# First feed-forward block: down products as seven block products over chunks of six features, norm factor on the gated features

## The chip, the core and the metric

The kernel runs on one core of a Trainium2 chip. Its engines work side by side, each with its own queue in order: TensorE (PE) multiplies matrices into PSUM, VectorE (DVE) and ScalarE (ACT) work element by element, GpSimd (POOL) here issues the DMAs that accumulate into SBUF, SyncE (SP) issues the others. The metric is the time of one execution in device microseconds; lower is better.

## What is computed

The reference is one step of a hybrid decoder: a first half-step SwiGLU block, a mixer (causal pooling beside a state-space part), a second half-step SwiGLU block and a last norm. There are 512 prompt tokens and 8 sample tokens, 520 in all, D_MODEL = 1024 and FFN_DIM = 2816, all in float32. Cut to what matters here:

```python
def _rms_norm(x, g):
    y = xf * lax.rsqrt(jnp.mean(xf * xf, axis=-1, keepdims=True) + EPS)
    return y * g
def _swiglu(x, wg, wu, wd):
    return (jax.nn.silu(x @ wg) * (x @ wu)) @ wd
...
h = h + 0.5 * _swiglu(_rms_norm(h, ffn1_norm[l]), ffn1_w_gate[l], ffn1_w_up[l], ffn1_w_down[l])
```

## The kernel before

Features lie on the 128 partitions and tokens along the free axis. A block of 128 rows is called a feature here: the model has 8 of them, the FFN 22 (f = 0 to 21). The 520 tokens are cut into two halves of 260. `h` (line 81) holds the residual stream in SBUF.

**A product in three matmuls.** Weights and inputs are split into a high part (rounded to fp32r) and a low part (what is left). `mm3` (line 122) adds high x high, high x low and low x high in PSUM, at lines 123, 126 and 127: three matmuls of 128x128 by 128x260. `split` (line 102) makes the parts: ScalarE casts the high part (line 107), VectorE subtracts for the low part (line 114). With `late`, half of the low part is made without VectorE: ScalarE writes the negated high part (line 110) and a DMA from POOL's queue adds the weights from memory onto it (line 111).

**Gate and up.** The norm's factor per token (`nx[3]`, tile `r_f`) isn't put on the input; the matmuls work on h times the norm's weights, and the factor is multiplied on behind. For each feature the gate and up rows form a 2x2 block matrix (gate or up; first or second four input blocks), and so does the input (first or second four blocks; token half). `product` computes the 2x2 by 2x2 product with seven block products instead of eight, numbered 1 to 7, each four input blocks x 3 = 12 matmuls: 84 a feature. `prep_pair` (line 191) makes the seven combinations of the input once, in the tiles `xth` and `xtl`. `load` (line 255) fetches the two weight rows of a feature and makes the combinations of weights: `s1` (line 266) and `s2` (267, 268), then splits the tiles whi/wlo (three buffers a tag) and shi/slo (two). The results gather in the PSUM tiles `A` (one bank, two buffers) and `BE` (two banks, two buffers); ScalarE copies four intermediate sums to `ac` (line 294) before the bank is accumulated further. `gates` (line 298) combines them, applies the factor and Silu and multiplies with one up half; `close` (line 305) does the other half after product 4, and splits the gated feature into `g` (lines 309, 310). `step` runs the products of a feature in the order 1, then product 4 and `close` of the feature before, then 5, 6, 3, 7, 2, then `gates`.

**The first two features** of the first block (f = 0 and 1) are done with plain float32 matmuls (`plain`, line 238) while the inputs arrive; `plain_out` gates them.

**Down.** `rest` goes over the features in chunks of 8, 8 and 6. One or two products of the next chunk's first features come ahead, so that TensorE has work while the last gated feature is split. `down` then takes each of the eight output row blocks d: one load of its weight rows over the chunk (`load_unit`), a split, 2 halves x n features x 3 matmuls into a `BE` tile (named `dn`), then VectorE multiplies with -0.5 and the norm factor (line 364, tile `td`) and adds to `h` (line 368; in the last chunk 371 for each half, followed by the preparation of the mixer's input). The down matmuls of the first block are 22 x 8 x 2 x 3 = 1056.

**Order.** The program is written in the order above; a planner sets the order on each engine by priority (program order, raised by `high_priority`) and by a timeline of its own. Tiles of one tag share buffers, and a new tile waits for the release of an old one. The second block has the same class, chunks of 8, 8 and 6 and another last chunk (`down_by_half`).

Of the kernel before, what the change touches and what calls it, by code (L numbers as in the profile page):

```python
# [33 lines left out]
CHUNKS = (8, 8, 6)  # L34
# [28 lines left out]
def tile_trunk_step(ctx: ExitStack, tc: tile.TileContext, ins: dict, outs: dict):  # L63
# [120 lines left out]
    def scaled(gp, nb, norm, j, name):  # L184
        xg = gp.tile([P, 4, HB], F32, tag="g", bufs=nb, name=f"xg_{name}{j}")
# [5 lines left out]
    def prep_pair(nx, gp, nb, xg, j, name):  # L191
        xth, xtl, _, _ = nx
        xd = gp.tile([P, 4, HB], F32, tag="g", bufs=nb, name=f"xd_{name}{j}")
# [10 lines left out]
    class Ffn:  # L204
# [4 lines left out]
        def __init__(self, nx, i, wx, gp, direct):  # L209
            self.nx, self.i, self.wx, self.gp, self.direct = nx, i, wx, gp, direct  # L210
            self.states = None
            self.w, self.A, self.BE, self.ac, self.g, self.tg, self.raw, self.banks, self.behind = ({} for _ in range(9))

# [12 lines left out]
        def plain(self, f, xg, j, us=(0, 1)):  # L226
            for u in us:
                if (f, u) not in self.banks:
                    n = f"P{self.i}_{f}{u}"
                    if f == 1 and u == 0:  # L230
# [10 lines left out]
        def plain_out(self, f):  # L241
            tg = self.wx.tile([P, 2, HB], F32, tag="tg", bufs=2, name=f"tg{self.i}_{f}")
            g = self.g[f] = self.gp.tile([P, 2, 2, HB], F32R, tag="g", bufs=NG, name=f"g{self.i}_{f}")
# [3 lines left out]
            nc.scalar.activation(out=tg, in_=tg, func=AF.Silu)  # L247
            for b in range(2):
                nc.vector.scalar_tensor_tensor(out=tg[:, b], in0=self.banks[f, 1][b][:, :HB], scalar=-1.0, in1=tg[:, b],
                                               op0=ALU.mult, op1=ALU.mult)  # L250
            nc.scalar.copy(g[:, 0], tg)
            nc.vector.tensor_tensor(out=g[:, 1], in0=tg, in1=g[:, 0].bitcast(F32), op=ALU.subtract)
            return free.ins

        def load(self, f):
            i, wx, src = self.i, self.wx, ins[f"w{self.i}gu"]
            n = f"{i}_{f}"
            raw = raw_pair(n)
            nc.sync.dma_start(out=raw[:, 0], in_=src[2 * f])
            nc.sync.dma_start(out=raw[:, 1], in_=src[2 * f + 1])  # L260
            d1 = split(raw[:, 0], 1024, f"{n}a", wp, 3, ("whi", "wlo"), src[2 * f, :, 512:])
            s1 = wx.tile([P, 2, 512], F32, tag="sw", bufs=2, name=f"s1_{n}")
            s2 = wx.tile([P, 2, 512], F32, tag="sw", bufs=2, name=f"s2_{n}")
            up0 = raw[:, 1, :512].unsqueeze(1).to_broadcast([P, 2, 512])
            diag = bass.AP(up0.tensor, up0.offset - 1024, [up0.ap[0], (1536, 2), up0.ap[2]])
            nc.vector.tensor_tensor(out=s1, in0=diag, in1=up0, op=ALU.add)  # L266
            nc.vector.tensor_tensor(out=s2[:, 0], in0=s1[:, 1], in1=raw[:, 0, :512], op=ALU.add)
            nc.vector.tensor_tensor(out=s2[:, 1], in0=s2[:, 0], in1=raw[:, 0, 512:], op=ALU.add)
            e1 = split(s1.rearrange("p q c -> p (q c)"), 1024, f"{n}c", wx, 2, ("shi", "slo"))
            e2 = split(s2.rearrange("p q c -> p (q c)"), 1024, f"{n}d", wx, 2, ("shi", "slo"))  # L270
            d2 = split(raw[:, 1, 512:], 512, f"{n}b", wp, 3, ("whi", "wlo"), src[2 * f + 1, :, 512:])
            self.w[f] = {1: (d1, 0), 2: (d1, 4), 7: (e1, 0), 5: (e1, 4), 6: (e2, 0), 3: (e2, 4), 4: (d2, 0)}

        def product(self, f, p):
            js = range(KD // 2)
            if f not in self.A:
                with tc.issue_after(self.behind[f]) if f in self.behind else nullcontext():
                    self.load(f)
                n = f"{self.i}_{f}"
                self.A[f] = ps[0].tile([P, 512], F32, tag="A", bufs=2, name=f"A{n}")  # L280
                self.BE[f] = ps[0].tile([P, 2, 512], F32, tag="BE", bufs=2, name=f"BE{n}")
                self.ac[f] = [self.wx.tile([P, 2, HB], F32, tag="ac", bufs=3, name=f"ac{n}_{q}") for q in range(2)]
            slot, dst, opens = {1: (0, 0, True), 2: (1, 1, True), 5: (3, 2, True), 6: (5, 0, False),
                                3: (2, 2, False), 7: (4, 0, False), 4: (6, 0, False)}[p]
            out = self.A[f] if dst == 0 else self.BE[f][:, dst - 1]
            (whi, wlo), k0 = self.w[f][p]
            xth, xtl = self.nx[:2]
            for j in js:
                mm3(out[:, :HB], ws(whi, k0 + j), ws(wlo, k0 + j), xth[:, j, slot], xtl[:, j, slot], opens and j == 0,
                    j == KD // 2 - 1, skip_group_check=True)  # L290
            a, c = self.ac[f]
# [6 lines left out]
        def gates(self, f):  # L298
            tg = self.tg[f] = self.wx.tile([P, 2, HB], F32, tag="tg", bufs=2, name=f"tg{self.i}_{f}")
            nc.vector.tensor_tensor(out=tg, in0=self.BE[f][:, :, :HB], in1=self.ac[f][0], op=ALU.add)  # L300
            nc.vector.tensor_tensor(out=tg, in0=tg, in1=self.nx[3].rearrange("p (b t) -> p b t", b=2), op=ALU.mult)
            nc.scalar.activation(out=tg, in_=tg, func=AF.Silu)
            nc.vector.tensor_tensor(out=tg[:, 1], in0=self.ac[f][1][:, 0], in1=tg[:, 1], op=ALU.mult)

        def close(self, f):
            tg = self.tg[f]
            nc.vector.tensor_tensor(out=tg[:, 0], in0=self.A[f][:, :HB], in1=tg[:, 0], op=ALU.mult)
            g = self.g[f] = self.gp.tile([P, 2, 2, HB], F32R, tag="g", bufs=NG, name=f"g{self.i}_{f}")
            nc.scalar.copy(g[:, 0], tg)  # L309
            nc.vector.tensor_tensor(out=g[:, 1], in0=tg, in1=g[:, 0].bitcast(F32), op=ALU.subtract)  # L310
# [3 lines left out]

        def rest(self, before, last_chunk):
            lo = 0
            for c, n in enumerate(CHUNKS):
                hi = lo + n
                last = hi == KF
                for f in range(self.direct if c == 0 else lo + 1, hi if last else hi + 1):  # L320
                    self.step(f)
                if last:
                    self.product(KF - 1, 4)
                    with tc.high_priority():
                        self.close(KF - 1)
                    wd = before()
                else:
                    self.product(hi + 1, 1)
                    self.product(hi, 4)
                    self.close(hi)  # L330
# [4 lines left out]
                lo = hi  # L335

        def step(self, f):
            if f not in self.A:
                self.product(f, 1)
            if f - 1 not in self.g and f > self.direct:  # L340
                self.product(f - 1, 4)
                self.close(f - 1)
# [772 lines left out]
```

## Time and profile before

| | |
|---|---|
| median of 3 runs | 1008.37 us (1007.89 to 1009.1) |
| profiled execution | 1008.41 us, of which the span is 1006.5 us |
| down products of the first block, in the span | 112 to 371 us |
| first seven-product feature of the second block begins | 651 us |
| HBM traffic | 127.36 MB read, 7.34 MB written |

In the profile, a row of a group reads: line, engine, operation, output tile <- input tiles, shapes, count | busy us, mean ns of one | idle time of the engine before them and who ended it. Rows of the timeline read: start, duration, engine, line, operation, tiles, shapes, and in brackets the idle time before it. Durations of TensorE and VectorE are pipelined: the next instruction can start before the last has ended, so the price of one is the distance between starts. Tile names carry the feature: `slo_5c` is the low part of the first weight sum of feature 5, `shi_5d` the high part of the second.

### The profile page before, as it was taken

What the parts mean: (1) busy time and instruction counts of PE and PEld (TensorE: products, weight loads), DVE (VectorE), ACT (ScalarE), POOL (GpSimd) and SP (SyncE); (2) the same over time, 40 slices, a digit from 0 to 9 for tenths busy, and PEclk for the clock granted to TensorE, in tenths of its full rate; (3) what the DMA queues carried; (4) which work ended last, traced back from release to release, by engine and by line L of the source; (5) the groups of instructions that cost most, each with busy time, mean ns of one, the idle gap of its engine ahead of it and who ended that gap; (6) DMA issues with size and microseconds to landing.
All of it is one profiled execution on the core that took longest, in us unless ns stands there. A gap on an engine that the chain in (4) does not pass through costs nothing.

```text
span 1006.5 us, 19720 instructions
## 1 busy us (share of the span) xinstructions
PE 976.0 (97%) x7852; PEld 952.8 (95%) x7852; DVE 766.7 (76%) x1366; ACT 564.4 (56%) x961; POOL 157.3 (16%) x239
## 2 busy tenths in 40 slices
PE   7999999999999999999999999999999999999996
PEld 6899999999999999999899998899999999999995
DVE  7788556886468688789979987998857788477776
ACT  7677415765137455685754325677644676535653
POOL 0111001110011000156411000111212211122100
PEclk9999999999999999999999999999999999999998
DMA  5566424754345332263335322456646766556612
GB/s 185 166 167 163 111 99 116 178 137 117 126 110 135 93 124 97 90 192 100 121 122 159 117 86 95 127 131 175 140 139 185 210 151 165 131 179 171 144 64 85
DMA packets 53835, 135.97 MB, mean 135 GB/s; under 512 B 7720, under 2 KB 14824, under 8 KB 53744
## 3 DMA queue, kind: packets, MB, share of 16 engines
q1 hardware_dynamic: 38864, 103.78, 31.8%
q0 software_dynamic: 14880, 30.94, 16.0%
q8 instruction: 61, 1.00, 0.4%
q14 instruction: 30, 0.25, 0.1%
HBM read 127.36 MB, written 7.34 MB: 134 GB/s over the span
## 4 chain that ended last, share of the span: by engine, by line
PE 85%; DVE 6%; ACT 5%; issue 2%; DMA 2%; POOL 1%; SPq 0%; DVEq 0%; ACTq 0%; POOLq 0%
PE A L123 8%; PE A L126 7%; PE A L127 7%; PE dn L127 7%; PE dn L123 6%; PE dn L126 6%; PE BE L123 6%; PE BE L127 6%; PE BE L126 6%; PE P L238 3%; PE wo L123 2%; PE wo L126 2%; PE wo L127 2%; PE inz L123 2%; PE inz L127 2%
## 5 line engine op out<-in xcount | busy, mean ns | idle before, releaser
L123 PE MATMUL dn<-g,whi_1d 128*128 128x260 f32 x352 | 99.5, 283 | 1.8 <-ACT whi_1d L107 1.6
L126 PE MATMUL dn<-g,whi_1d 128*128 128x260 f32 x352 | 99.5, 283 | 0.0
L127 PE MATMUL dn<-g,wlo_1d 128*128 128x260 f32 x352 | 99.0, 282 | 0.0
L364 DVE SCALAR_TENSOR_TENSOR td<-dn,r_f 128x520 f32<-128x520 f32 x40 | 27.9, 699 | 91.7 <-PE dn L127 91.7
L127 PE MATMUL dn<-g,wlo_2d 128*128 128x260 f32 x256 | 72.8, 284 | 2.0 <-DVE wlo_2d L114 2.0
L123 PE MATMUL dn<-g,whi_2d 128*128 128x260 f32 x256 | 72.4, 283 | 0.1
L126 PE MATMUL dn<-g,whi_2d 128*128 128x260 f32 x256 | 72.3, 282 | 0.0
L123 PEld LDWEIGHTS dn<-g,whi_1d 128*128 128x128 f32 x352 | 66.1, 188 | 2.4 <-ACT whi_1d L107 2.0
L126 PEld LDWEIGHTS dn<-g,whi_1d 128*128 128x128 f32 x352 | 66.3, 188 | 0.0
L127 PEld LDWEIGHTS dn<-g,wlo_1d 128*128 128x128 f32 x352 | 66.1, 188 | 0.0
L107 ACT CAST whi_1d<-raw_1d 128x1024 fp32r<-128x1024 f32 (+1 forms) x24 | 23.4, 979 | 70.4 <-PE dn L126 62.2
L294 ACT COPY ac<-A 128x260 f32<-128x260 f32 x123 | 44.0, 371 | 17.1 <-PE A L127 17.1
L266 DVE TENSOR_TENSOR s<-raw 128x1024 f32<-128x1024 f32 x41 | 49.9, 1218 | 3.3 <-DMA raw<-in_w2gu 3.3
L238 PE MATMUL P<-xg_f,raw 128*128 128x260 f32 x192 | 45.6, 396 | 5.3 <-DMA raw<-in_w1gu 5.3
L127 PEld LDWEIGHTS dn<-g,wlo_2d 128*128 128x128 f32 x256 | 48.2, 188 | 2.6 <-DVE wlo_2d L114 2.6
L123 PEld LDWEIGHTS dn<-g,whi_2d 128*128 128x128 f32 x256 | 48.3, 189 | 0.3 <-ACT whi_2d L107 0.3
L126 PEld LDWEIGHTS dn<-g,whi_2d 128*128 128x128 f32 x256 | 48.2, 188 | 0.0
L238 PEld LDWEIGHTS P<-xg_f,raw 128*128 128x128 f32 x192 | 37.4, 198 | 11.2 <-ACT xg_f L187 5.2
L126 PE MATMUL wo<-catg,whi_wo 128*128 128x260 f32 x128 | 36.4, 285 | 1.3 <-DVE catg L972 1.3
L123 PE MATMUL wo<-catg,whi_wo 128*128 128x260 f32 x128 | 37.3, 292 | 0.3 <-DVE h L941 0.3
L310 DVE TENSOR_TENSOR g<-tg,g 128x520 fp32r<-128x520 f32 x41 | 28.6, 698 | 11.6 <-ACT g L309 11.6
L123 PE MATMUL inz<-xh_mx,whi_inz 128*128 128x260 f32 x128 | 36.8, 287 | 0.1
(1442 smaller groups left out, 4001.2 us busy)
## 6 DMA issues: line engine op xcount, KB each, us to landing
raw<-in_w2gu SPq DMA_DIRECT2D x44, 512.0 KB, 4.7
raw<-in_w1gu SPq DMA_DIRECT2D x42, 512.0 KB, 4.5
raw_1d<-in_w1d SPq DMA_DIRECT2D x16, 512.0 KB, 4.4
raw_2d<-in_w2d SPq DMA_DIRECT2D x16, 512.0 KB, 5.7
raw_wo<-in_w_out SPq DMA_DIRECT2D x12, 512.0 KB, 4.5
ab<-scr_acs SPq DMA_DIRECT2D x8, 512.0 KB, 4.4
h<-in_state_ssm SPq DMA_DIRECT2D x16, 256.0 KB, 4.1
raw_inz<-in_w_in SPq DMA_DIRECT2D x8, 512.0 KB, 4.3
```

The source lines that it names most:

```text
L107: nc.scalar.copy(h, src)
L123: first = nc.tensor.matmul(ps, whi, xhi, start=start, stop=False, **kw)
L126: nc.tensor.matmul(ps, whi, xlo, start=False, stop=False, **kw)
L127: nc.tensor.matmul(ps, wlo, xhi, start=False, stop=stop, **kw)
L238: nc.tensor.matmul(self.banks[f, u][b][:, :HB], ws(self.raw[f][:, u], j + 4 * q), xg[:, slot[q]], start=j == q == 0, stop=j == 3 and q == ...
L266: nc.vector.tensor_tensor(out=s1, in0=diag, in1=up0, op=ALU.add)
L294: nc.scalar.copy(keep, out[:, :HB])
L310: nc.vector.tensor_tensor(out=g[:, 1], in0=tg, in1=g[:, 0].bitcast(F32), op=ALU.subtract)
L364: nc.vector.scalar_tensor_tensor(out=t, in0=banks[d][:, :, :HB], scalar=-0.5, in1=self.nx[3].rearrange("p (b t) -> p b t", b=2), op0=ALU.mult,
```

## The change

The down products of the first block are done in chunks of six, three times, and a last chunk of four. In the chunks of six, two output row blocks d and d+1 and the two halves of the chunk's features (first three, last three) form a 2x2 block matrix, as gate and up do, and the features by token halves the other; the same seven products give both output blocks, 7 x 3 x 3 matmuls for what took 2 x 2 x 6 x 3. Such a unit (c, d) passes through the same `load`, `product`, `gates` and `close` as a feature; its columns are 768 instead of 1024. Features of a chunk are taken in pairs (0 and 3, 1 and 4, 2 and 5), and after the second of a pair is closed `g_split` makes the seven combinations of the pair and splits them into a tile `gt` (14 parts, three buffers). The first of a pair keeps its gated values in the tile tagged `acc`. The plain features are 0 and 3.

The norm factor and the 0.5 move: each gated feature is multiplied with the factor once more, and the eviction of the down products only adds or subtracts. The last chunk of four stays with plain down products. Input tiles of the plain features move to a pool `xo` of their own, which is released before the pool of the gated features opens. The second block has `paired` = 0, its chunks as before.

```diff
-CHUNKS = (8, 8, 6)
+CHUNKS = {1: (6, 6, 6, 4), 2: (8, 8, 6)}
...
+        def role(self, f):
+            c = self.chunk[f]
+            fs = self.chunks[c]
+            if c < self.paired:
+                return ("first", "second")[fs.index(f) % 2]
+            return "late" if 0 < c <= self.paired and f == fs[0] else "plain"
+
+        def g_homes(self, f):
+            t = self.tg[f]
+            if self.role(f) in ("first", "late"):
+                t = act.tile([P, NT], F32, tag="acc", name=f"gx{self.i}_{f}").rearrange("p (b t) -> p b t", b=2)
+                self.gx = t
+            self.out[f] = t
...
+        def g_split(self, f):
+            role = self.role(f)
+            if role == "plain":
+                self.g_plain(f, self.out[f])
+            if role != "second":
+                return
+            gx, go = self.gx, self.out[f]
+            self.gx = None
+            t = self.gt[f] = self.gp.tile([P, 14, HB], F32R, tag="gt", bufs=3, name=f"gt{self.i}_{f}")
+            xd = self.gp.tile([P, 4, HB], F32, tag="xd", name=f"gd{self.i}_{f}")
+            nc.vector.tensor_tensor(out=xd[:, 0], in0=gx[:, 0], in1=gx[:, 1], op=ALU.subtract)
+            nc.vector.tensor_tensor(out=xd[:, 1], in0=go[:, 1], in1=gx[:, 1], op=ALU.subtract)
+            nc.vector.scalar_tensor_tensor(out=xd[:, 2], in0=xd[:, 1], scalar=-1.0, in1=gx[:, 0], op0=ALU.mult,
+                                           op1=ALU.subtract)
+            nc.vector.scalar_tensor_tensor(out=xd[:, 3], in0=xd[:, 2], scalar=-1.0, in1=go[:, 0], op0=ALU.mult,
+                                           op1=ALU.subtract)
+            for x, q in ((gx[:, 0], 0), (go, slice(1, 3)), (xd, slice(3, 7))):
+                hi, lo = t[:, 0:7][:, q], t[:, 7:14][:, q]
+                nc.scalar.copy(hi, x)
+                nc.vector.tensor_tensor(out=lo, in0=x, in1=hi.bitcast(F32), op=ALU.subtract)
...
+            if self.paired:
+                nc.vector.tensor_tensor(out=tg, in0=tg, in1=self.halves(self.nx[3]), op=ALU.mult)
...
+            if isinstance(k, tuple):
+                c, d = k
+                fs = self.chunks[c]
+                n, src = f"{i}d{d}_{c}", ins[f"w{i}d"][d : d + 2, :, min(fs) * P : (max(fs) + 1) * P]
+            else:
+                n, src = f"{i}_{k}", ins[f"w{i}gu"][2 * k : 2 * k + 2]
+            nb = src.shape[2] // 2
...
+            n = len(self.chunks[k[0]]) // 2 if isinstance(k, tuple) else KD // 2
+            for j in range(n):
+                if isinstance(k, tuple):
+                    t = self.gt[self.chunks[k[0]][2 * j + 1]]
+                    xhi, xlo = t[:, slot], t[:, 7 + slot]
...
+            nc.vector.tensor_tensor(out=tg, in0=self.BE[k][:, :, :HB], in1=a, op=ALU.add)
+            if isinstance(k, tuple):
+                hd, hn = h[:, k[1]], h[:, k[1] + 1, HALVES[1]]
+                nc.vector.tensor_tensor(out=hd, in0=hd, in1=tg.rearrange("p b t -> p (b t)"), op=ALU.add)
+                nc.vector.tensor_tensor(out=hn, in0=hn, in1=c[:, 0], op=ALU.subtract)
+                return
...
+            if self.paired:
+                nc.vector.tensor_tensor(out=tg, in0=tg, in1=r, op=ALU.mult)
+            self.up(k, 1, c[:, 0])
...
+        def close(self, k):
+            if isinstance(k, tuple):
+                hn = h[:, k[1] + 1, HALVES[0]]
+                nc.vector.tensor_tensor(out=hn, in0=hn, in1=self.A[k][:, :HB], op=ALU.subtract)
+                return
+            self.up(k, 0, self.A[k][:, :HB])
+            self.g_split(k)
...
+                if c < self.paired:
+                    for d in range(0, KD, 2):
+                        self.step((c, d))
+                    continue
...
+        def step(self, k):
+            if k not in self.A:
+                self.product(k, 1)
+            self.flush()
+            for p in (2, 5, 6, 3, 7) if k == KF - 1 else (5, 6, 3, 7, 2):
+                self.product(k, p)
+            self.gates(k)
+            self.pending = k
...
+                if self.paired:
+                    if after is None:
+                        nc.vector.tensor_tensor(out=hd, in0=banks[d][:, :, :HB], in1=hd, op=ALU.add)
+                        return
+                    for b, hs in enumerate(HALVES):
+                        nc.vector.tensor_tensor(out=h[:, d, hs], in0=banks[d][:, b, :HB], in1=h[:, d, hs], op=ALU.add)
+                        after(d, b, hs)
+                    return
...
-    wx1, g1 = pool("wx1", "right"), pool("g1", "right")
+    wx1, xo = pool("wx1", "right"), pool("xo", "left")
...
-    ffn1 = Ffn(nx1, 1, wx1, g1, 2)
+    ffn1 = Ffn(nx1, 1, wx1, None, 2, 3)
...
+    xo.release()
+    g1 = ffn1.gp = pool("g1", "right")
```

`flush` runs product 4 and `close` of the feature or unit before; `up` multiplies a gated half with an up half (with -0.5 in the first block); `g_plain` splits one feature as `close` did before.

More of the change, by code (lines that the diff above doesn't have):

```diff
@@ L253, in plain_out @@
+            self.g_split(f)
             return free.ins
-        def load(self, f):
-            i, wx, src = self.i, self.wx, ins[f"w{self.i}gu"]
-            n = f"{i}_{f}"
-            raw = raw_pair(n)
[L259 to L272, printed above, removed]
@@ L312, in scales, with flush @@
         def scales(self):
             rstds(self.nx, f"f{self.i}")
-        def rest(self, before, last_chunk):
[L316 to L320, printed above, removed]
-                    self.step(f)
+        def flush(self):
+            if self.pending is not None:
+                self.product(self.pending, 4)
+                self.close(self.pending)
+                self.pending = None
@@ L459, in tile_trunk_step @@
         for j in range(KD // 2):
-            ffn1.plain(1, xg1[j], j, (u,))
+            ffn1.plain(second, xg1[j], j, (u,))
+    xo.release()
+    g1 = ffn1.gp = pool("g1", "right")
     with tc.high_priority():
-        ffn1.behind[2] = ffn1.plain_out(0)
-    ffn1.plain_out(1)
+        ffn1.behind[ffn1.order[2]] = ffn1.plain_out(0)
+    ffn1.plain_out(second)
     nx2, xa = [], []
```

162 lines of the change are left out of this document (101 added, 61 removed).

## The prediction

> **What bounds the kernel now.** I read the page from the top, then the stretches of the first block by window, then one feature step on VectorE instruction by instruction.
>
> ```profile
> span 1006.5 us, 19720 instructions
> PE 976.0 (97%) x7852; PEld 952.8 (95%) x7852; DVE 766.7 (76%) x1366; ACT 564.4 (56%) x961; POOL 157.3 (16%) x239
> ...
> PEclk9999999999999999999999999999999999999998
> ...
> L123 PE MATMUL dn<-g,whi_1d 128*128 128x260 f32 x352 | 99.5, 283 | 1.8 <-ACT whi_1d L107 1.6
> ```
>
> TensorE is busy for 97% of the span at the full granted clock, so a matmul removed is time removed, unless another engine then runs out. The first block's down products are 1056 matmuls: this group of 352 and its two equals from lines 126 and 127 (three matmuls make one product). Their 283 ns is a pipelined duration; the price of one is the distance between starts:
>
> ```profile
> 362.89 0.70 DVE L364 SCALAR_TENSOR_TENSOR td<-dn,r_f 128x520 f32<-128x520 f32 x1 [0.20 <-PE dn L127]
> ...
> 367.20 0.70 DVE L364 SCALAR_TENSOR_TENSOR td<-dn,r_f 128x520 f32<-128x520 f32 x1 [0.53 <-PE dn L127]
> ```
>
> These two evictions follow the 36 matmuls of one output row block each (6 features x 2 halves x 3): 4.31 us / 36 = 0.120 us. The next view says how full the engines are (PE, PEld, DVE, ACT, POOL, clock, DMA share, GB/s): a stretch of feature steps, the two passages from feature steps to down products, and a stretch of down products.
>
> ```profile
> 65.00:89.00 24.00, 24.00 (x202) 24.00 (x201) 20.50 (x29) 16.78 (x29) 4.33 (x5) 1.00 0.65 155
> 107.00:124.00 17.00, 15.55 (x125) 14.93 (x125) 8.77 (x12) 6.54 (x10) 0.87 (x1) 1.00 0.32 82
> 124.00:150.00 26.00, 26.00 (x219) 26.00 (x219) 12.08 (x15) 4.20 (x4) 0.00 (x0) 1.00 0.33 120
> 236.00:254.00 18.00, 16.55 (x133) 15.93 (x132) 8.70 (x12) 6.54 (x10) 0.87 (x1) 1.00 0.35 97
> ```
>
> In the feature steps TensorE has no idle time at all, and VectorE is already busy for 85% (20.50 of 24). In the down products VectorE is half idle. At each passage TensorE stands for 1.45 us. The VectorE queue over one feature step:
>
> ```profile
> 64.95 1.23 DVE L114 TENSOR_TENSOR slo_5c<-s,shi_5c 128x1024 fp32r<-128x1024 f32 x1 [1.14 <-ACT shi_5c L107]
> 66.10 0.69 DVE L300 TENSOR_TENSOR tg<-BE,ac 128x520 f32<-128x520 f32 x1
> 66.71 1.22 DVE L266 TENSOR_TENSOR s<-raw 128x1024 f32<-128x1024 f32 x1
> 67.84 0.70 DVE L301 TENSOR_TENSOR tg<-tg,r_f 128x520 f32<-128x520 f32 x1
> 68.45 1.22 DVE L114 TENSOR_TENSOR slo_5d<-s,shi_5d 128x1024 fp32r<-128x1024 f32 x1
> 69.58 0.43 DVE L296 TENSOR_TENSOR ac<-ac 128x260 f32<-128x260 f32 x1
> 69.92 0.69 DVE L267 TENSOR_TENSOR s<-s,raw 128x512 f32<-128x512 f32 x1
> 70.53 0.43 DVE L303 TENSOR_TENSOR tg<-ac,tg 128x260 f32<-128x260 f32 x1
> 71.21 0.43 DVE L307 TENSOR_TENSOR tg<-A,tg 128x260 f32<-128x260 f32 x1 [0.26 <-PE A L127]
> 71.55 0.68 DVE L268 TENSOR_TENSOR s<-s,raw 128x512 f32<-128x512 f32 x1
> 72.17 0.69 DVE L114 TENSOR_TENSOR wlo_6a<-raw,whi_6a 128x512 fp32r<-128x512 f32 x1
> 73.22 0.70 DVE L310 TENSOR_TENSOR g<-tg,g 128x520 fp32r<-128x520 f32 x1 [0.36 <-ACT g L309]
> 75.06 1.23 DVE L114 TENSOR_TENSOR slo_6c<-s,shi_6c 128x1024 fp32r<-128x1024 f32 x1 [1.14 <-ACT shi_6c L107]
> ```
>
> The step takes 75.06 - 64.95 = 10.11 us, which is 84 matmuls x 0.120. VectorE idles 0.26 + 0.36 + 1.14 = 1.76 us of it and works 8.35. That 1.76 us is what the change has to live on.
>
> **The change part by part.**
>
> *Matmuls.* A pair of output blocks over six features took 2 x 2 x 6 x 3 = 72 matmuls and takes 7 x 3 x 3 = 63. Four pairs in three chunks: 12 x 9 = 108 fewer, x 0.120 = **13.0 us off**. The last chunk of four stays as it was, 24 matmuls a block. Gate and up products and the whole second block keep their counts.
>
> *The passages.* These rows say what TensorE waits for between 95 and 255 us:
>
> ```profile
> PE dn L123 <- ACT whi_1d L107: 1.6, 2, 0.8
> PE A L123 <- ACT ac L294: 1.4, 4, 0.4
> ```
>
> They come about because products 1 and 4 of the features at the edge run back to back, and because the down weights join the rotation of the weight buffers there. After the change a down unit passes through the same step as a feature, product by product, so both passages should close: 2 x 1.45 = **2.9 us off**; the other end is that nothing closes, 0. The passage into the last chunk remains.
>
> *VectorE in the feature steps.* Each feature gets one more multiplication by the norm factor (a row like L301, 0.61 us from start to start: 67.84 to 68.45). Each pair loses two L310 rows (0.70 each, drained) and gains four sums and three low parts. Their prices stand in the preparation of the input, which does the same work:
>
> ```profile
> 20.25 0.42 DVE L196 SCALAR_TENSOR_TENSOR xd_f<-xd_f,xg_f 128x260 f32<-128x260 f32 x1
> 20.59 1.24 DVE L202 TENSOR_TENSOR xtl_f<-xd_f,xth_f 128x1040 fp32r<-128x1040 f32 x1
> 21.74 0.43 DVE L198 SCALAR_TENSOR_TENSOR xd_f<-xd_f,xg_f 128x260 f32<-128x260 f32 x1
> ```
>
> A 260 costs 0.34, a 1040 1.15, a 520 0.61: 4 x 0.34 + 0.34 + 0.61 + 1.15 = 3.46 us. A pair of steps: 2 x 8.35 - 2 x 0.70 + 2 x 0.61 + 3.46 = 19.98 us against 20.22 us of TensorE. VectorE is then 99% full. The work is not due at once, though: the split of a pair is first read by the down products, and its feature's buffer is needed again two steps later. What is due is the weights' low part. These rows of TensorE, one step earlier, say when:
>
> ```profile
> 58.26 0.28 PE L127 MATMUL BE<-xth_f,slo_4c 128*128 128x260 f32 x1
> ...
> 59.34 0.28 PE L127 MATMUL BE<-xth_f,slo_4c 128*128 128x260 f32 x1
> ...
> 61.15 0.28 PE L123 MATMUL BE<-xth_f,shi_4d 128*128 128x260 f32 x1
> ```
>
> slo_5c ends at 66.18 and its first reader, a step after slo_4c's, starts at 58.26 + 10.11 = 68.37; so it may come 2 us late. The split falls into the flush after L307, at 71.55: laid out there it moves slo_6c by about 1 us, and the following step, which has no split, takes this back. Bounds for a pair: 0, if the order is that good, and 2.5 us, if all of the present idle time but the 0.36 and a little more stays (below). I take 0.3, near the lower end because of the 2 us; 8 pairs in steps: **2.4 us on**.
>
> *VectorE and ScalarE in a down unit.* It carries the weight sums of a feature step over 768 columns: 1.13 x 3/4 = 0.87 for the first sum and for each of two low parts, 0.46 for the two halves and the short low part, then 0.34 (c), 0.61 + 0.61 + 0.34 + 0.34 to combine and add to h: 6.2 us, in 63 x 0.120 = 7.56 us. That share, 82%, is what feature steps carry today with no idle TensorE. Before it was L364, L368 and one low part a block. But the gaps in which ScalarE must empty a bank shrink by a quarter:
>
> ```profile
> 69.81 0.38 ACT L294 COPY ac<-BE 128x260 f32<-128x260 f32 x1 [0.32 <-PE BE L127]
> ```
>
> In the TensorE rows above, between the last matmul of product 5 and the first of product 3 into the same bank lie 1.81 us (59.34 to 61.15), less 0.28 for its end: 1.53 us for this 0.38 us copy. In a unit three matmuls fewer lie between, 1.17 us. Bounds: 0 and 0.6 us a unit (a cast in front of the copy each time); I take 0.15, as it fits if ScalarE has no cast going; 12 units: **1.8 us on**.
>
> *DMA and queues.* SyncE issues two weight loads a unit, as for a feature (8 loads a chunk as before, in four chunks instead of three), and POOL two accumulating loads that the down products did not have:
>
> ```profile
> 66.76 0.87 POOL L111 DMA_DIRECT2D wlo_5b<-in_w1gu  x1 [3.03 <-ACT wlo_5b L110]
> ```
>
> A feature step issues two of these as well, and its DMA share of 0.65 leaves TensorE without a wait; a unit moves three quarters of the bytes in three quarters of the time. I cost it at nothing. The cover is the 7.56 us of the unit before, by which the loads run ahead; without it a unit would start late by what a load lacks. POOL, at 16%, has nothing queued behind.
>
> *The last chunk.* A block falls from 4.31 to 24 x 0.120 = 2.88 us. VectorE worked 4.31 - 0.20 - 0.53 = 3.58 us in the period shown above; it loses L364 (0.61) and a third of a 768 low part (0.29): 2.68 of 2.88. Two banks allow one block of lateness, and in-projection starts on early blocks. Bounds 0 and 2; I take **0.6 us on**.
>
> *Start.* The plain steps now do features 0 and 3 and free their input tiles before the new buffers open. Two more factors and one split land where VectorE had nothing to do, 0 within 1 us:
>
> ```profile
> 40.07 0.69 DVE L114 TENSOR_TENSOR wlo_3a<-raw,whi_3a 128x512 fp32r<-128x512 f32 x1 [1.79 <-ACT whi_3a L107]
> ```
>
>
> **Sum**, against the profiled execution's 1008.4 us (1006.5 in the span and 1.9 around it; the median of the runs is 1008.37): 1008.4 - 13.0 - 2.9 + 2.4 + 1.8 + 0.6 = **997.3 us**.
>
> **Rivals.**
>
> *VectorE becomes the bound (slower).* The place is the pair of feature steps. If the waits of a step that are tied to the order of the products (0.26 and 1.14) stay where they are, a pair needs 19.98 + 2.8 = 22.8 us, 2.6 over TensorE. 8 x 2.6 = 21 in place of 2.4: 1008.4 - 15.9 + 21 + 2.4 = 1016. It decides from (15.9 - 2.4) / 8 = 1.7 us a pair upward. For it: 99% is no margin, and the queue runs in order. Against: those idles exist because nothing else was ready; the split is ready work. Chance 0.10.
>
> *Each instruction pays its full duration.* The twelve durations of the step shown add up to 9.11 us. A pair is then 18.22 - 1.40 + 1.40 + (5 x 0.42 + 0.70 + 1.24) = 22.3 us, 2.0 over TensorE: 1008.4 - 15.9 + 16 + 2.4 = 1011, slower too. Against it: slo_5c starts at 64.95 and lasts 1.23, yet the next row starts at 66.10, 0.08 before its end, and so do nearly all. For it: the three sums of a split that hang on each other do wait in full. Chance 0.04. The Trainium skill ("VectorE: DVE Perf Modes", "The DRAIN you can't avoid") states this rule: the next VectorE operation starts only when the one before has left the pipe, so that the count of operations is to be kept small. By that rule the time would be the 1011 of this rival; the trace agrees only in part, with the 0.08 us.
>
> *The split is laid badly,* 1.2 us a pair: 9.6 for 2.4, 1004.5. For it: in the flush it comes ahead of weight parts that are due sooner. Chance 0.07.
>
> *ScalarE's copies are late in the units:* 0.6 x 12 = 7.2 for 1.8: 1002.7. For it: every unit leaves a quarter less room, and casts of the split join the queue. Against: ScalarE has 56% to do. Chance 0.12.
>
> *All hides:* 1008.4 - 15.9 = 992.5. The feature steps of today show no idle TensorE at 85%. Chance 0.12.
>
> *The passages stay* (the 2.9 remain, or the down units wait for the last split instead): 1000.2; it lies in the forecast's own range and has its chance there.
>
> **How the numbers follow.** The forecast, 994 to 1001.5, has 0.55. With "all hides", the ScalarE case and the badly laid split, 992 to 1005 would hold 0.86; of that some 0.04 falls outside at the two ends. A difference of 0.2%, 2.0 us, is about what can be told from no change. Faster than 1006.4: 0.55 + 0.12 + 0.12 + 0.04 = 0.83. Within: 0.03, the rest of the badly laid split. Slower: 0.10 + 0.04 = 0.14.
>
> **What would show it.** The down matmuls of the first block fall to 192, with 756 in the new units; the unit repeats every 7.6 us and the feature pair every 20.2. The two windows of passages show TensorE full. VectorE in the feature steps reads 95% or more. If a feature pair takes 21 us or more with TensorE waiting for slo or wlo, the first rival holds; if units take over 8 us with waits for ac, the ScalarE one. The prediction would be wrong if TensorE's idle time in the first block passed 10 us, or if a step of the second block changed its length.

## The result and the profile after

The changed kernel takes 999.08 us (median of 4 runs, 996.41 to 999.47) against 1008.25 us for the kernel before (4 runs, one more than in the table above); ratio 0.9902, 95% interval 0.9884 to 0.992. That is 9.2 us faster; 11.1 us were forecast, and the time lies in the range. The profiled execution of the changed kernel took 999.47 us, 997.6 of them in the span.

The page of the changed kernel, its span, engines and clock:

```profile
span 997.6 us, 19913 instructions
PE 963.4 (97%) x7744; PEld 939.7 (94%) x7744; DVE 826.2 (83%) x1509; ACT 614.5 (62%) x1074; POOL 178.5 (18%) x263
...
PEclk9999999999999999999999999999999999999998
```

There are 7852 - 7744 = 108 matmuls fewer, as counted, and VectorE works 60 us more at a share of 83% instead of 76%. What became of the down products, by groups of TensorE's instructions (the first from 36 to 372 us, the second from 84 to 124 us):

```profile
L123 PE MATMUL dn<-gt,whi_1d 128*128 128x260 f32 x64 | 18.1, 285 | 0.8 <-ACT gt L248 0.6 <-DVE h L474 0.3
```

```profile
L123 PE MATMUL A1d<-gt,whi_1d_0a 128*128 128x260 f32 x12 | 3.5, 292 | 0.2 <-DVE gx L395 0.2
```

64 in each of the three lines of a product, 192 in all, are the plain products of the last chunk; the second group shows the first line of one product, over the four units of a chunk (3 pairs x 4).

Two marks in the chain of waits let the gain be placed: the norm sum that ends the first block, and the last input preparation before the second. Before:

```profile
376.09 0.44 PE psr_mx L169 x2
...
647.11 1.06 ACT xth_f L201
```

After:

```profile
365.68 0.44 PE psr_mx L169 x2
...
635.79 1.06 ACT xth_f L202
```

So 10.4 us come from the first block; at the second mark the lead is 11.3 us; at the end it is 1006.5 - 997.6 = 8.9. In the second block, whose instructions did not change, 2.4 us are lost again. There TensorE waits longer for down weights; before, and after (engine, waited for: us in total, times, longest):

```profile
PE dn L127 <- DVE wlo_2d L114: 2.0, 3, 0.8
```

```profile
PE dn L127 <- DVE wlo_2d L114: 4.5, 4, 1.7
```

The first block by stretches, after (TensorE, weight load, VectorE, ScalarE, GpSimd busy; clock; DMA share; GB/s):

```profile
44.00:84.00 40.00, 40.00 (x334) 40.00 (x334) 38.03 (x59) 29.00 (x49) 6.93 (x8) 1.00 0.60 145
84.00:94.00 10.00, 8.73 (x70) 8.29 (x69) 9.87 (x19) 6.66 (x11) 1.73 (x2) 1.00 0.52 118
94.00:124.00 30.00, 29.72 (x245) 29.32 (x245) 25.36 (x41) 21.03 (x40) 6.06 (x7) 1.00 0.70 172
164.00:187.00 23.00, 22.24 (x182) 21.83 (x181) 21.33 (x36) 15.98 (x29) 4.33 (x5) 1.00 0.53 119
187.00:216.00 29.00, 29.00 (x245) 29.00 (x244) 25.91 (x43) 20.47 (x38) 6.06 (x7) 1.00 0.71 175
256.00:280.00 24.00, 23.24 (x190) 22.83 (x190) 22.18 (x38) 16.54 (x30) 4.33 (x5) 1.00 0.54 120
336.00:370.00 34.00, 31.51 (x255) 30.14 (x254) 28.49 (x63) 21.50 (x47) 0.73 (x3) 1.00 0.32 107
```

In feature steps (44 to 84) VectorE is 95% busy and TensorE has no idle time. In the units (187 to 216) none either. TensorE stands at the three passages into the units, 1.27 + 0.28, 0.76 and 0.76 us, and in the last chunk, 2.49 us. Its waits from the first block to the start of the mixer, by what ended them:

```profile
PE BE1d L123 <- ACT gt L269: 1.0, 1, 1.0
PE BE1d L126 <- DVE gt L270: 0.9, 2, 0.5
PE BE1d L123 <- ACT ac1d L367: 0.8, 3, 0.3
PE dn L123 <- ACT gt L248: 0.6, 1, 0.6
PE dn L126 <- DVE gt L249: 0.3, 1, 0.3
PE dn L123 <- DVE h L474: 0.3, 1, 0.3
PE dt L752 <- DVE dt_v L772: 1.4, 1, 1.4
```

The 2.49 us of the last chunk fall into two places: 0.58 + 0.29 + 0.26 = 1.13 us at its start, for the split of a feature and an eviction, and 1.36 us at its end, where the mixer's first product `dt` waits while VectorE, busy for 15.78 of 16 us from 346 to 362, is behind with the evictions and the mixer's input. The kernel before has the same two places, with 0.20 and 0.88 us. Before:

```profile
345.34 0.39 PE L123 MATMUL dn<-g,whi_1d 128*128 128x260 f32 x1 [0.20 <-DVE td L364]
372.36 0.29 PE L635 MATMUL dt<-xh_mx,w 128*48 128x260 f32 x1 [0.88 <-DVE td L364]
```

After, the first wait of the start and the one at the end:

```profile
340.56 0.50 PE L123 MATMUL dn<-gt,whi_1d 128*128 128x260 f32 x2 [0.58 <-ACT gt L248]
361.96 0.29 PE L752 MATMUL dt<-xh_mx,w 128*48 128x260 f32 x1 [1.36 <-DVE dt_v L772]
```

At the passages the waits of before, for whi_1d and ac at the edge, are gone. The new ones are for gt, the split of the last gated pair, and 0.28 us each for the first unit's copy ac1d. VectorE's queue at the first passage shows why the split is late:

```profile
84.03 0.42 DVE L395 SCALAR_TENSOR_TENSOR tg<-A,tg 128x260 f32<-128x260 f32 x1
84.37 0.42 DVE L262 TENSOR_TENSOR gd<-tg,gx 128x260 f32<-128x260 f32 x1
...
88.83 0.42 DVE L265 SCALAR_TENSOR_TENSOR gd<-gd,tg 128x260 f32<-128x260 f32 x1
...
90.38 0.69 DVE L389 TENSOR_TENSOR tg<-tg,r_f 128x520 f32<-128x520 f32 x1
...
92.60 1.23 DVE L270 TENSOR_TENSOR gt<-gd,gt 128x1040 fp32r<-128x1040 f32 x1
```

The pair is closed at 84.03. The last of the four sums runs at 88.83 and the last low part at 92.60, 8.6 us later, for the split shares the queue with the sums and low parts of the first down weights and with the gate of the next feature. From 84 to 94 us VectorE is busy for 9.87 of 10. ScalarE adds to the first wait: the last sum is done at 89.25, but its cast starts at 90.89, behind a cast of weights that starts at 90.15.

### The profile page after: what moved, and what is told of

The parts are those of the page before. It is cut to its first block, busy times and chain, and to the rows that moved or that the text cites. A ratio compares the mean times of both kernels' runs of the same rounds, so it can differ in the third digit from the quotient of the medians.

```text
span 997.6 us, 19913 instructions
## 1 busy us (share of the span) xinstructions
PE 963.4 (97%) x7744; PEld 939.7 (94%) x7744; DVE 826.2 (83%) x1509; ACT 614.5 (62%) x1074; POOL 178.5 (18%) x263
## 4 chain that ended last, share of the span: by engine, by line
PE 81%; DVE 8%; DMA 4%; ACT 3%; issue 2%; POOL 0%; SPq 0%; DVEq 0%; ACTq 0%; POOLq 0%
PE A L123 7%; PE A L126 7%; PE A L127 7%; PE BE L123 6%; PE BE L126 6%; PE BE L127 6%; PE P L296 3%; PE dn L127 2%; PE wo L123 2%; PE dn L126 2%; PE dn L123 2%; PE wo L126 2%; PE wo L127 2%; PE inz L123 2%; DMA raw<-in_w2gu 2%
## 5 line engine op out<-in xcount | busy, mean ns | idle before, releaser
L478 DVE SCALAR_TENSOR_TENSOR td<-dn,r_f 128x520 f32<-128x520 f32 x16 | 11.2, 698 | 32.6 <-PE dn L127 32.6
L107 ACT CAST whi_2d<-raw_2d 128x1024 fp32r<-128x1024 f32 (+1 forms) x18 | 18.5, 1027 | 31.5 <-PE dn L126 16.7
L123 PE MATMUL inx<-xh_mx,whi_inx 128*128 128x260 f32 x128 | 36.4, 284 | 0.0
L127 PE MATMUL wo<-catg,wlo_wo 128*128 128x260 f32 x128 | 36.3, 284 | 0.0
L127 PE MATMUL inx<-xh_mx,wlo_inx 128*128 128x260 f32 x128 | 36.2, 283 | 0.0
L127 PE MATMUL inz<-xh_mx,wlo_inz 128*128 128x260 f32 x128 | 36.2, 283 | 0.0
L126 PE MATMUL inz<-xl_mx,whi_inz 128*128 128x260 f32 x128 | 36.1, 282 | 0.0
L126 PE MATMUL inx<-xl_mx,whi_inx 128*128 128x260 f32 x128 | 36.1, 282 | 0.0
L957 ACT ACTIVATE so<-br,sxdt 128x128 f32<-128x128 f32 x64 | 20.5, 391 | 25.2 <-DMA br<-scr_bc 18.7
```

What stands on the lines that cost most here:

```text
L107: nc.scalar.copy(h, src)
L123: first = nc.tensor.matmul(ps, whi, xhi, start=start, stop=False, **kw)
L126: nc.tensor.matmul(ps, whi, xlo, start=False, stop=False, **kw)
L127: nc.tensor.matmul(ps, wlo, xhi, start=False, stop=stop, **kw)
L478: nc.vector.scalar_tensor_tensor(out=t, in0=banks[d][:, :, :HB], scalar=-0.5, in1=self.nx[3].rearrange("p (b t) -> p b t", b=2), op0=ALU.mult,
L957: nc.scalar.activation(out=o[:, q], in_=br, func=AF.Copy, scale=sxdt[:, j, b : b + 1]))
```

## The experiments

All medians are of runs beside the kernel before on the same chip. Where a run is set against the changed kernel, the changed kernel's own ratio, 0.9902 and 0.9916 in two measurements, is the measure.

**The norm factor alone.** Chunks of 8, 8 and 6, plain products, the factor on the gated features:

```diff
-CHUNKS = {1: (6, 6, 6, 4), 2: (8, 8, 6)}
+CHUNKS = {1: (8, 8, 6), 2: (8, 8, 6)}
...
-            if self.paired:
+            if self.factor:
                 nc.vector.tensor_tensor(out=tg, in0=tg, in1=r, op=ALU.mult)
...
-    ffn1 = Ffn(nx1, 1, wx1, None, 2, 3)
+    ffn1 = Ffn(nx1, 1, wx1, None, 2, 0, True)
```

> Only the norm factor moves onto the gated features; chunks of 8, 8 and 6 and plain down products as before. My theory: a feature step gets 0.61 us of VectorE more (8.35 to 8.96 of 10.1 us), which fits, and a down block loses one eviction of 0.70 us, which was hidden; TensorE's 1056 down matmuls stay, so the time is that of before, 1008.4 within 1.5 us. Rival, the factor itself costs time on a VectorE that is full: 20 features x 0.61 = 12 us slower, 1020. Second rival, the shorter eviction is what gained: 2 to 4 us faster than before.

Measured: 1008.08 us, ratio 0.9992 (0.9983 to 1.0001). By itself this part changes nothing, as the theory had it; the gain belongs to the rest of the change, the units of seven products with their smaller chunks.

**Without the sample states, before and after.** Two runs to separate the second block:

```diff
-    f2["ffn"].states = f2["states"](f2["st"])
-    next(f2["ffn"].states)
```

> The kernel before, leaving out the update of the sample states during the second block (its loads and stores, ScalarE and VectorE work; that output is not written). My theory: the second block, 354.6 us from its first seven-product feature to the end in the trace of before, loses its waits for late weights, 2.0 us or a little more; 1003 to 1007. It is the partner of the next run.

> The changed kernel, leaving out the same update of the sample states. My theory: the 11.3 us that the changed kernel is ahead when the second block begins stay to the end, since the 2.4 us it loses there come from weight loads colliding with the states' DMAs: 11.3 us (10.5 to 12) less than the run without states of the kernel before, and the second block of both equally long within 0.3 us. Rival, the second block itself became slower by the edit: the difference stays 8.9 us.

Measured: 1006.34 us (0.9977, 0.9967 to 0.9987) and 996.34 us (0.9876, 0.9861 to 0.989): 10.0 us apart. The second marks of the two, of the kernel before without states and of the changed one without states:

```profile
647.67 1.06 ACT xth_f L201
```

```profile
637.19 1.06 ACT xth_f L202
```

From there to the ends of the spans (1004.9 and 994.4 us) both take 357.2 us. The lead of 10.5 us at the mark stays to the end. So in this pair of traces the loss in the second block is gone with the states' transfers; the edit doesn't slow that block itself. The difference of the medians, 10.0 us, lies below the 10.5 to 12 that were expected and above the 8.9 of the rival.

**The changed kernel once more.**

> The changed kernel once more. My theory: the first block and the mixer take the same time again to 0.3 us (mixer's start at the same point of the span), and what differs between executions, 996.4 to 999.5 us, lies in the second block, in the waits for wlo of the down weights (4.5 us in the first trace). Rival: the executions differ in the first block.

Measured: 1000.71 us (997.79 to 1001.06), ratio 0.9916 (0.99 to 0.9932). Its norm sum stands at 367.23 us instead of 365.68; the difference is in the start, where TensorE waits 0.8 us for whi_4a, among others. Its second block takes 361.3 us, that of the first trace 361.8, both longer than the 359.4 of the kernel before; in the traces of the runs below, whose edits lie in the first block, it took 360.0 to 364.2. So executions differ in both places, and the expectation that the first block repeats to 0.3 us was wrong.

**More work for VectorE, on the gate's chain.** Once and twice more:

```diff
             nc.vector.tensor_tensor(out=tg, in0=self.BE[k][:, :, :HB], in1=a, op=ALU.add)
+            for _ in range(1 if self.paired and not isinstance(k, tuple) else 0):
+                nc.vector.tensor_tensor(out=tg, in0=self.BE[k][:, :, :HB], in1=a, op=ALU.add)
```

> The changed kernel with the addition of BE and ac (a 520-column VectorE instruction, 0.61 us from start to start) done a second time in every feature step of the first block. My theory: the changed kernel still has about 1.0 us of idle VectorE in a pair of steps (38.03 of 40 us busy), so 1.22 us a pair overflow by 0.2, with a little at each passage: 1 to 6 us slower than the changed kernel. Rival, VectorE is the bound already: 20 x 0.61 = 12 us slower.

> The same addition done twice more. My theory: 2.44 us a pair against 1.0 of room: 8 pairs x 1.45 = 11.6 us and 3 passages x 1.2: 12 to 18 us slower than the changed kernel, with TensorE waiting for slo or wlo in the feature steps. Rival, VectorE is the bound already: 24 us slower. Third, VectorE has room that the busy share doesn't show: under 6 us.

Measured: 1014.63 us (1.0057, 1.004 to 1.0073) and 1033.4 us (1.024, 1.0222 to 1.0257), some 15 and 33 us over the changed kernel. Both are beyond the theory, and even beyond the price of the instructions (12 and 24). The trace of the first run shows a second effect: the repeat doesn't follow the first addition, it runs 3.5 us later and makes the whole gate late.

```profile
68.34 0.70 DVE L379 TENSOR_TENSOR tg<-BE,ac 128x520 f32<-128x520 f32 x1
...
71.89 0.70 DVE L381 TENSOR_TENSOR tg<-BE,ac 128x520 f32<-128x520 f32 x1
```

They do show, with the trace of the first, where it hurts: the waits for gt at the passages grow to 6.4 and 2.2 us. Two of these waits, at the second and third passage, last 3.2 us each, and a third effect follows: TensorE's granted clock falls behind them, to 0.88 and 0.89 over these stretches (TensorE, weight load, VectorE, ScalarE, GpSimd busy; clock; DMA share; GB/s):

```profile
187.00:216.00 29.00, 24.68 (x182) 24.35 (x181) 22.20 (x38) 16.50 (x33) 5.18 (x6) 0.88 0.49 112
280.00:310.00 30.00, 25.69 (x190) 25.27 (x190) 23.52 (x42) 17.07 (x33) 4.32 (x5) 0.89 0.50 122
```

That alone is an estimated 0.12 x 29 + 0.11 x 30 = 6.8 us of the 15; in the second run three such stretches (0.94 from 94 to 124 us, 0.88 from 187 to 216, 0.93 from 310 to 336) are worth about as much. Without the clock the two runs lose some 8 and 26 us, around the price of the instructions. A pair of feature steps grew only from 20.2 to 20.7 us in the first run, which is near the theory (0.2 over) and not the rival (1.2): most of the loss is at the passages. So these runs mix load, delay and clock, and don't give the price of VectorE's work by itself.

**More work off the chain.** Two 260-column multiplications a step into a tile that nobody reads:

```diff
+            for q in range(2 if self.paired and not isinstance(k, tuple) else 0):
+                t = tmp.tile([P, HB], F32, tag="ta", name=f"more{n}{q}")
+                nc.vector.tensor_tensor(out=t, in0=r[:, 0], in1=r[:, 1], op=ALU.mult)
```

> The changed kernel with two more 260-column VectorE multiplications in every feature step of the first block, into a tile that nobody reads: 2 x 0.34 = 0.68 us of VectorE a step, and off the chain of the gate, which the repeated addition of the earlier run had lengthened (it ran 3.5 us behind the first one). Theory, a queue that is nearly full: 1.36 us a pair against 1.0 of room, so little in the feature steps and 2 to 3 us at each of the three passages, where the split falls due: 5 to 11 us slower than the changed kernel. Rival, all of it costs: 20 x 0.68 = 14 us. Rival, only the longer chain cost: under 3 us.

Measured: 1015.83 us, ratio 1.0068 (1.0046 to 1.0089). The planner, free to place them, ran them in bunches of three in the first steps (44 to 74 us). Most of the loss sits there, with the clock described at the end, while later steps keep their 10.1 us. The first passage, shortly behind the bunches, suffers too: TensorE waits there for 2.0 and 0.9 us, and the clock is 0.89 from 94 to 124 us. At the other passages nothing was added, and they are as in the changed kernel. The run is inconclusive for the question it was made for.

**Less work for VectorE.** The factor's multiplication is left out:

```diff
-            if self.paired:
-                nc.vector.tensor_tensor(out=tg, in0=tg, in1=r, op=ALU.mult)
```

> The changed kernel, leaving out the multiplication of the gated features with the norm factor in the first block (its results are scaled wrongly), 0.61 us of VectorE less in every feature step. Theory, the waits for gt at the passages come from a full VectorE queue: TensorE's 2.8 us of idle time at the three passages falls under 1 us, the feature steps stay at 10.1 us, and the kernel is 1.5 to 3 us faster than the changed one. Rival, the waits come from the length of the split's own chain: within 0.7 us.

Measured: 995.22 us, ratio 0.9868 (0.9852 to 0.9885), about 4 us faster than the changed kernel in time. In the trace more is gained: the norm sum stands at 360.14 us, against 365.68 to 367.23 in four executions whose order of work is that of the changed kernel. Its first two passages:

```profile
84.00:94.00 10.00, 10.00 (x86) 10.00 (x85) 8.52 (x14) 7.68 (x15) 1.73 (x2) 1.00 0.57 125
...
164.00:187.00 23.00, 23.00 (x194) 23.00 (x193) 20.56 (x35) 16.63 (x30) 4.65 (x6) 1.00 0.59 123
```

TensorE no longer stands at any passage, and the low part that came at 92.60 starts 6.4 us sooner:

```profile
86.19 1.23 DVE L270 TENSOR_TENSOR gt<-gd,gt 128x1040 fp32r<-128x1040 f32 x1
```

The factor stood in the gate's chain too, and 3.0 of these 6.4 us come from the pair being closed sooner (81.06 instead of 84.03), 3.4 from the split itself. What a passage costs in full is seen from product 4 of the feature before the chunk's end to product 4 of the second feature of the next chunk, across the down units: 420 matmuls in both traces (count, durations, first and last start). The changed kernel, for the second passage:

```profile
L123 PE MATMUL A<-xth_f,whi_11b x4: 282/282/285, 173.1 to 174.2; 128*128 128x260 f32 x4
...
L123 PE MATMUL A<-xth_f,whi_15b x4: 283/284/288, 224.7 to 225.8; 128*128 128x260 f32 x4
```

Without the factor:

```profile
L123 PE MATMUL A<-xth_f,whi_11b x4: 283/284/288, 170.1 to 171.2; 128*128 128x260 f32 x4
...
L123 PE MATMUL A<-xth_f,whi_15b x4: 283/284/287, 220.5 to 221.6; 128*128 128x260 f32 x4
```

51.6 us against 50.4, which is 420 x 0.120: this passage costs 1.2 us, of which 0.76 shows as idle TensorE; the rest is in restarts, since a matmul after a wait is shown longer (0.39 us instead of 0.28) and covers part of the gap. The first passage (features 5 to 9) takes 53.0 us against 50.3, the third (17 to 19) 51.6 against 50.4. Together they cost 5.1 of the 5.5 us. The theory holds against its rival (the split's own chain), and it was too small: the same instruction that costs nothing alone takes some 5 us at the passages beside the split. By itself this run doesn't part a full queue from the shorter chain of the gate, nor from the order that the planner chose anew; the run with the factor on GpSimd, below, has more to say on that.

**The split first.** High priority for the last pair's split:

```diff
-            self.g_split(k)
+            last = self.paired and self.role(k) == "second" and k == self.chunks[self.chunk[k]][-1]
+            with tc.high_priority() if last else nullcontext():
+                self.g_split(k)
```

> The changed kernel with the split of the last pair of each chunk of six put ahead in the planner's order (high priority). My theory: at the three passages into the down units TensorE waits for gt (1.0 + 0.9 us by the waits) and stands 0.8 to 1.3 us each; with the split first these waits go and 1.5 to 3 us are gained. Rival, VectorE is full there and whatever is put back makes TensorE wait instead: within 0.7 us.

Measured: 1000.95 us, ratio 0.9919 (0.99 to 0.9937), no gain. But VectorE's instructions at the first passage come in the same order as without the edit, so the split wasn't put first and the question wasn't put to the chip.

**More cover in the last chunk.** A third block ahead of the last split, in two spare banks:

```diff
                 part(1, range(n - 1))
-                part(0, range(n - 1, n))
-                done(0)
-                part(1, range(n - 1, n))
-                done(1)
-                first = 2
+                part(2, range(n - 1))
+                for d in range(3):
+                    part(d, range(n - 1, n))
+                    done(d)
+                first = 3
```

> The changed kernel with a third output block taken ahead of the last feature's split in the last chunk (its weights in the shi/slo buffers, its sums in two spare PSUM banks). My theory: the last chunk's start stands 1.5 to 2.5 us because the cover ahead of the last gated feature fell from 2 x 2 x 5 x 3 = 60 matmuls (7.2 us) to 2 x 2 x 3 x 3 = 36 (4.3 us); 18 more matmuls (2.2 us) give back 1 to 1.7 us. Rival, it waits for the down weights instead: nothing, or a loss of up to 1 us.

> The changed kernel with a third output block ahead of the last feature's split, once more: 2 to 4 us faster than the changed kernel, 995.5 to 998.

Measured: 996.9 us (0.9883, 0.9862 to 0.9904) and again 997.26 us (0.988, 0.9862 to 0.9898). In the trace of the first the waits for gt of the last chunk (0.6 and 0.3 us) are gone and the norm sum stands at 364.03 us, 1.6 us sooner than in the changed kernel's first trace. The wait at the end of the chunk stays (0.21 + 1.24 us). The intervals overlap those of the changed kernel; by the ratios it is 2 to 3 us ahead of it.

**The factor on GpSimd,** with that cover:

```diff
-                nc.vector.tensor_tensor(out=tg, in0=tg, in1=r, op=ALU.mult)
+                nc.gpsimd.tensor_tensor(out=tg, in0=tg, in1=r, op=ALU.mult)
```

> As the run before, and the norm factor is multiplied onto the gated features by GpSimd instead of VectorE. Theory: VectorE loses 0.61 us a feature step and the waits for gt at the passages go: 1 to 2.5 us faster than the run before. Rival, GpSimd takes 1 to 2 us for it (a 512-column product of the mixer takes it 1.0 to 2.0 us) and its queue issues the accumulating loads, so gate and split come later and the passages get longer: 1 to 4 us slower than the run before.

Measured: 997.65 us, ratio 0.9887 (0.9872 to 0.9902), the same as with VectorE. The waits for gt are gone, but TensorE now waits 1.4 us for slo_1d_0d and 1.0 us for ac, so that the first passage still takes 52.9 us and the second 51.3, against 50.3 and 50.4 without the factor. Both theories were half right. The run helps to tell chain, order and load apart. The factor is still in the gate's chain, and the pair is closed no sooner than before (84.72). The split's sums now follow right behind it, and its last low part starts at 89.79. But VectorE is no less busy: 38.44 of 40 us from 124 to 164 us, against 37.84 with the factor on it, because some of its instructions take longer beside GpSimd's (see the end). So with the split ahead on a VectorE that stays full, other work is late in its place, as the rival of "The split first" had it. In these runs the passages close only where VectorE has less to do.

## Why the prediction was right, point by point

- **The matmuls, 13.0 us off:** right in count, and the units run at TensorE's rate without idle time behind their first one. With the factor left out, the first block ends 5.5 us before that of the changed kernel, 16 us before that of the kernel before. That this is the 15.9 us of the case "all hides" is in part chance: there the passages gave more than the 2.9, as the next point shows, and the last chunk took some back.
- **The passages, 2.9 us off:** this step failed as the prediction put it ("both passages should close"). The old waits closed, but TensorE stands 1.55 + 0.76 + 0.76 = 3.1 us at three passages instead of 2.9 at two. In full, by the matmuls' starts, the three cost 2.6 + 1.2 + 1.2 = 5.0 us over 0.120 a matmul. The two of the kernel before cost 2.1 and 2.4: from product 4 of feature 5 to that of feature 11 it takes 108.7 us, from 13 to 19 109.0, for 888 matmuls each (106.6). So the passages are 0.5 us on instead of 2.9 off. It is what the rival "the passages stay" named, the down units waiting for the last split; it had been put inside the forecast's range at 1000.2, near the 999.08 measured.
- **VectorE in the feature steps, 2.4 us on:** nothing there. Steps stay at 10.1 us with VectorE at 95%. The ledger of 99% was near the truth, but its price was not paid where the work is done. It was paid where the work falls due, at the passage. So the cost was placed wrongly, and the reason given (the split is ready work that can wait) was the very reason it arrived late.
- **Units, 1.8 us on:** none within a chunk's units. The three waits of 0.28 us for ac1d come at the first unit of each chunk and are counted at the passages.
- **The last chunk, 0.6 us on:** mis-sized. From product 4 of feature 19 (at 317.6 before, 316.7 after) to the norm sum it takes 49.0 us instead of 58.5, 9.5 less, where 96 fewer matmuls are 11.5: 2.0 us on, of which 1.4 show as idle TensorE, 0.9 at the start and 0.5 at the end. For the start the prediction missed the cover: 36 matmuls instead of 60 ahead of the last gated feature. The third block ahead shows this. The end is near its own worry, VectorE's load per block (2.68 of 2.88 us); no run tested it.
- **The second block** was held unchanged. Its instructions are, but with the states' transfers it took 2.4 and 1.9 us longer in the two traces of the changed kernel. Why the transfers fall worse, at the same order of work on TensorE, VectorE and ScalarE from the mixer on, stays open; in the pair of traces without them the loss was absent.
- **The rivals:** VectorE as the bound of the feature steps, by waits that stay or by full durations, did not come about. How near it was, the runs with added work show only in part, since the one lengthened a chain and lost clock and the other was placed elsewhere.

Terms as they turned out, to the first mark: -13.0, + 0.5 at the passages, + 2.0 in the last chunk: 10.5 off, with 10.4 measured. Set against the prediction's own terms, the passages came out 3.4 us worse and the last chunk 1.4 worse, the feature steps and units 4.2 better. These misses nearly cancel, and so, less closely, do the 0.9 us that the mixer gained and the 2.4 that the second block lost. The matmuls were understood; that the sum came within 2 us of the time is in part luck.

## What to carry to other kernels

Work that may be late isn't free on an engine that is 95% full: ask at which point it falls due, and what stands ahead of it in the queue there. Two edits that each cost nothing alone can cost together, so the cheap one should be tried beside the expensive one too. When a chunk gets smaller, count again what covers its first dependency, not only what each block costs.

## What the runs showed of the hardware

**Behind some waits TensorE's clock halved.** With the added work off the chain TensorE stood for 3.1 us in one wait. In the matmuls behind it (start, duration, engine, line) the distance grows from 0.12 us to 0.22:

```profile
67.36 0.32 PE L127 MATMUL A<-xth_f,wlo_2a 128*128 128x260 f32 x1
67.48 0.42 PE L123 MATMUL A<-xth_f,whi_2a 128*128 128x260 f32 x1
67.70 0.42 PE L126 MATMUL A<-xtl_f,whi_2a 128*128 128x260 f32 x1
67.92 0.42 PE L127 MATMUL A<-xth_f,wlo_2a 128*128 128x260 f32 x1
```

In that stretch, and in the next (TensorE busy, clock, DMA share, GB/s), the granted clock is 0.53, then 0.98; the third line is an earlier stretch of the same trace:

```profile
67.00:74.00 7.00, 6.46 (x29) 0.53 0.33 76
74.00:84.00 10.00, 10.00 (x83) 0.98 0.41 105
44.00:47.00 3.00, 3.00 (x16) 0.50 0.62 132
```

The Trainium skill ("TensorE: Matmul & The Clock Gate", "Part 1: The HAM clock gate") says that an idle window of about 3.4 us sends TensorE back to half its clock until a busy one has passed; this case agrees only in part. The clock also fell behind shorter waits: in this trace it is 0.50 from 44 to 47 us, behind waits of 1.4 and 0.3 us, and 0.51 from 105 to 112 us, behind 2.0 and 0.9. Behind the changed kernel's waits at its passages, 1.03 us at most, it stayed at 1.00. How long TensorE has to stand, and how the gaps add up, these runs don't show.

**GpSimd beside VectorE.** With the factor on GpSimd, its 520-column product took from 1.3 to 4.1 us, and a VectorE instruction that takes 0.55 us elsewhere took 1.70 beside one. First the range over all twenty, then the pair:

```profile
L389 POOL TENSOR_TENSOR tg<-tg,r_f x20: 1307/1487/4086, 53.2 to 335.0; 128x520 f32<-128x520 f32 x20
```

```profile
82.27 1.31 POOL L389 TENSOR_TENSOR tg<-tg,r_f 128x520 f32<-128x520 f32 x1 [4.39 <-ACT tg L386]
```

```profile
82.29 1.70 DVE L335 TENSOR_TENSOR s_1d<-s_1d,raw_1d 128x384 f32<-128x384 f32 x1
```

Both begin at 82.3 and VectorE's ends 0.41 us after GpSimd's, as if it had waited for the other to finish. So moving work from a full VectorE to an idle GpSimd gave back what it took off: VectorE's busy time from 124 to 164 us even grew, from 37.84 to 38.44 us.
